# A two-layer network in fp32: the seven products per pair in another order, results formed in PSUM, a ninth piece of W, and the mixing, transposes and returns laid out by rows

## The chip, the cores and the metric

The kernel runs on one core of one Trainium2 chip. The time is the device time of one execution in microseconds. Before the change it is 2397.4 us, the median of two runs (2396.65 and 2398.15).

## The reference, cut to what matters

512 tokens of width 2048 pass through two layers. Layer 0 (forgetting attention and an RWKV-7 mixer) isn't touched. Layer 1 and the gate that closes it are:

```python
xn = rms_norm(h, norm_pre[i])
proj = xn @ c_w_in[j]                       # 512x2048 @ 2048x6144
u, v, g = _split(proj, (GMLP_W, GMLP_W, GMLP_W))
oc = chunked_spatial_gating(u, v, ...)      # below
y = (oc * jax.nn.silu(g)) @ c_w_out[j]
h = h + rms_norm(y, norm_post[i])
h = h + (p[i] @ ple_w_proj[i]) * jax.nn.sigmoid(h @ ple_w_gate[i])

# chunked_spatial_gating: 4 chunks of 128 tokens, 16 groups of 128 channels
u = gelu(u); v = layer_norm(gelu(v), ln_g, ln_b)
mixed = einsum('gts,bnsgc->bntgc', w_s * causal, vc) + b_s
return u * mixed
```

All of it is fp32 and the result must keep fp32's precision.

## The kernel before, in words

**Precise products.** Each fp32 operand is split into a high part `hi` (a ScalarE cast to the reduced format) and a low part `lo` (VectorE, the difference), and each product takes three matmuls: hi·hi, hi·lo, lo·hi. The two casts of a weight block are `whi` (line 1303) and `wlo` (line 1304) in the products that this change touches; four buffers of each lie between them and TensorE.

**Seven products.** `h @ W` of layer 1 and the last gate `h @ ple_w_gate` are done by a Strassen-Winograd scheme (`seven`, line 1309). The 512 tokens are split in two halves of 256, the 2048 input channels in two halves, and two column blocks of 512 of W form a `Pair`. Instead of eight quarter products there are seven, numbered 1 to 7, each of 8 k-steps of 128 channels; a k-step is 6 matmuls of 128x128 by 128x512 (lines 1324 to 1326), a product 48. Token-side sums (A11, A12, A22, S1 to S4) are formed once by `sets` (line 1203). Weight-side sums are formed in place, in `pieces` of W (two k-steps, 512 KB, line 1251):

- 1 loads W11 and, where `keep` is set, leaves it in `pr.E`; 2 loads W21.
- 5 adds W12 to E by an accumulating DMA that GpSimd issues (line 1281).
- 6 loads W22 into `pr.H` and adds it to E on VectorE (line 1267); 3 uses H as it is.
- 7 adds W12 to H by an accumulating DMA (line 1292); 4 loads W21 once more into a piece of its own and adds it to E on VectorE.

`piece` and `gone` (lines 1241 to 1249) take pieces from a queue `raws` of eight buffers and put them back at its end. Products 1 and 2 share one accumulator in PSUM, as do 5 and 3; all accumulators, transposes and mixing results come from the eight PSUM banks named `mm`. After each product `seven` copies or combines accumulators into SBUF tiles named `comb` (four, lines 1331 to 1351) and hands each finished 128x512 result to `pr.emit`.

**Order.** `FIRST` (line 74) orders the 14 products of two interleaved pairs: b1, a1, b2, a2, then 5, 6, 3, 7, 4 of a, and the same of b. `NEXT` (line 78) orders one pair alone: 1, 5, 2, 6, 3, 7, 4. In `layer_c` (line 1366) the columns of v come first (V, 14 products, `FIRST`), then U0, G0, U1, G1 (seven each, `NEXT`): u of the first 1024 channels, its gate g, and the same of the other half. In `last_layer` (line 1101) the gate `ple_w_gate` is 14 products in the order of `FIRST`. A label such as G0.2 is product 2 of G0; a and b are the two pairs of a `FIRST`.

**Emits of layer 1.** `vals` (line 1375) applies Gelu, collects the layer norm's statistics and stores v to DRAM (`vd`) on SyncE's queue. `gates` applies Gelu into `u[n]`, `silu` (line 1390) multiplies Silu(g) into it, and for the first half stores it to DRAM (`yd2`). `mix` (line 1399) does one group's spatial mixing: three small loads into the one buffer `accq` and a load of v's group into an `sq` tile, normalising by four ScalarE instructions (line 1411), the mask and two multiply-adds on GpSimd (lines 1406, 1414, 1415), a transpose of the mixing weight (line 1417), the casts of the weight (1419) and of v (1423, 1424) into `sg` tiles, three matmuls (1427 to 1429) and the multiplication into `u` (1431). `done` (line 1463), called after each product, calls two mixes after each of the first four products of G0 and G1, and in G1 also `early` (line 1458): load four blocks of y from `yd2`, transpose them on TensorE and split them (`operands`, line 1442). The other eight `operands` come after the last product, ahead of `c_w_out`.

**The last layer.** `post_norm` (line 989) runs `c_w_out` through `dense_all` (line 970) and forms the norm's factor; the `filler` meanwhile runs `p @ ple_w_proj`, copies each result through an `sg` tile (line 1133) and stores it to DRAM (`pd`, line 1134). `late` then updates h and `flip` (line 1152) turns it to token rows, 16 times: four transposes (line 1156), a copy into an `sg` tile (line 1158), a store to DRAM (`rd`, line 1159). Only then come the token-side sums and the 14 products; `emit` (line 1173) loads the matching tiles of `pd` and `rd` (lines 1183, 1184), applies the sigmoid, multiplies, adds and stores the output (line 1188).

**What sets the order.** The code is written as a flow of tiles. A planner gives each engine one fixed order of instructions, by program order as priority, by its own estimate of when operands and buffers are there, and by `high_priority` blocks (the casts of W and the additions of pieces stand in one). On the chip each engine and each queue works through its order strictly and waits on semaphores. All plain DMAs are issued by SyncE's queue (SP); the accumulating ones by GpSimd.

Of the kernel before, what the change touches and what calls it, by code (L numbers as in the profile page):

```python
# [16 lines left out]
P = 128  # L17
T = 512
# [51 lines left out]
def f(ap):  # L70
# [3 lines left out]
FIRST = lambda a, b: [  # L74
    (b, 1, False), (a, 1, True), (b, 2, True), (a, 2, True),
    *[(pr, n, True) for pr in (a, b) for n in (5, 6, 3, 7, 4)],
]
NEXT = 1, 5, 2, 6, 3, 7, 4


class Pair:


    def __init__(self, W, c0, n, emit):
        self.W, self.c0, self.n, self.emit = W, c0, n, emit
        self.E, self.H, self.acc, self.R = {}, {}, {}, {}


class Net:
# [899 lines left out]
    def post_norm(self, wap, gname, ops, keep, ps, wp, early, filler, kts=None):  # L989
# [3 lines left out]
        for n, acc in self.dense_all(wap, 0, ops, ps, 3, None, kts):  # L993
# [11 lines left out]
    def run(self):  # L1005
        tc = self.tc
        with ExitStack() as ctx:
# [12 lines left out]
            self.homes = {}  # L1020
            self.ahead = {}
# [6 lines left out]
    def rest(self, cp):  # L1028
        nc, tc, i = self.nc, self.tc, self.i
        npre, npost = self.cols["norm_pre"], self.cols["norm_post"]  # L1030
        with ExitStack() as ctx:
# [66 lines left out]
            pops = self.layer_c(cp, sets, accq, after, wp, ps)  # L1098
            self.last_layer(cp, pops, wp, ps)

    def last_layer(self, cp, yops, wp, ps):
# [36 lines left out]
        self.post_norm(i["c_w_out"][0], npost[:, 16:32], yops, keep, ps, wp, early, filler())  # L1138
# [13 lines left out]
        def flip(g, m):  # L1152
# [6 lines left out]
            nc.sync.dma_start(self.rd[:, m, g * T : (g + 1) * T], o)  # L1159

        def late(q):
            update(q, 1)
            update(q + 4, 1)
            if q % 2:
                for g in (q // 2, q // 2 + 2):
                    for m in range(4):
                        flip(g, m)

        sets = self.sets(A11, H, ps, wp, lambda q: (("yh", 2 * q + 8), ("yh", 2 * q + 9)), False, late)

        spare = []

        def emit(pr, m, n, src, cs=slice(0, T)):
            sg = src
            if not spare:
                for j in (2, 3):
                    tl = self.t(self.xp, [P, 4, T], f"xh{j}")
                    spare.extend(tl[:, q, :] for q in range(4))
            if (m, n % 2) in ((0, 0), (1, 0)):
                sg = self.t(wp, [P, T], "sg")  # L1180
            pj, res = self.t(wp, [P, T], "sq"), spare[0]
            spare.append(spare.pop(0))
            nc.sync.dma_start(pj, self.pd[:, m, n * T : (n + 1) * T])
            nc.sync.dma_start(res, self.rd[:, m, n * T : (n + 1) * T])
            nc.scalar.activation(sg, src, AF.Sigmoid)
            nc.vector.tensor_tensor(sg, sg, pj, ALU.mult)
            nc.vector.tensor_tensor(res, res, sg, ALU.add)
            nc.sync.dma_start(self.out[0, m * P : (m + 1) * P, n * T : (n + 1) * T], res)
# [3 lines left out]
        self.seven(FIRST(*pairs), sets, ps)  # L1192
# [10 lines left out]
    def sets(self, A11, xs, ps, wp, place, copy, late=lambda q: None):  # L1203
# [7 lines left out]
        A22, S3 = [[], []], [[], []]  # L1211
# [4 lines left out]
        for q in range(4):  # L1216
# [13 lines left out]
            self.part(S3, q, t)  # L1230
            src = xs[q + 4, 1]
            if copy:
                src = tmp("sg")
                nc.scalar.copy(src, xs[q + 4, 1])
            for e, (k, n) in enumerate(place(q)):
                A22[e].append(pair(k, n))
            self.part(A22, q, src)
        return {1: A11, 2: A12, 3: S4, 4: A22, 5: S1, 6: S2, 7: S3}

# [8 lines left out]
    def gone(self, tl):  # L1248
        self.raws.append(self.homes.pop(id(tl))[0])

    def pieces(self, pr, prod, keep):
# [8 lines left out]
        def load(*where):  # L1260
            tl = self.piece()
            nc.sync.dma_start(view(tl), block(*where))
            return tl

# [4 lines left out]
        for j in range(4):  # L1269
# [7 lines left out]
            elif prod == 5:  # L1277
# [3 lines left out]
                nc.gpsimd.dma_start(view(tl), block(0, 1, j), accum_op=ALU.add)  # L1281
# [6 lines left out]
            elif prod == 3:  # L1288
                tl = pr.H[j]
            elif prod == 7:  # L1290
                tl = done = pr.H.pop(j)
                nc.gpsimd.dma_start(view(tl), block(0, 1, j), accum_op=ALU.add)
            else:
# [3 lines left out]
                self.gone(g)  # L1297
# [11 lines left out]
    def seven(self, order, sets, ps, after=lambda n: None):  # L1309


        nc = self.nc
        for step, (pr, prod, keep) in enumerate(order):
# [4 lines left out]
            hs, ls = sets[prod]  # L1318
            for k, hi, lo in self.pieces(pr, prod, keep):
                for m in range(2):  # L1320
                    ms = slice(m * P, (m + 1) * P)
                    xh, xl = hs[k // 2][:, k % 2, ms], ls[k // 2][:, k % 2, ms]
                    more = dict(skip_group_check=True)
                    nc.tensor.matmul(acc[m], xh, hi, start=(first and k == 0), stop=False, **more)  # L1324
                    nc.tensor.matmul(acc[m], xh, lo, start=False, stop=False, **more)  # L1325
                    nc.tensor.matmul(acc[m], xl, hi, start=False, stop=(k == 7), **more)  # L1326
            tile = lambda: self.t(self.rp, [P, 2, T], "comb")
            for m in range(2):
                a = acc[m]
                if prod in (1, 5):  # L1330
                    if m == 0:
                        pr.R[prod] = tile()
                    nc.scalar.copy(pr.R[prod][:, m], a)
# [5 lines left out]
                elif prod == 7:  # L1339
                    if m == 0:  # L1340
                        pr.R[7] = tile()
                    u2, u3, c22 = (pr.R[x][:, m] for x in (1, 7, 5))
                    nc.vector.tensor_tensor(u3, a, u2, ALU.add)
# [432 lines left out]
```

## Time and profile before

| what | value |
|---|---|
| median of the runs | 2397.4 us |
| the profiled execution, its own time | 2392.33 us |
| its span, first to last instruction | 2390.6 us |
| mean granted clock | 0.972 |
| V's first product starts | 1384.6 us |
| first matmul of `c_w_out` | 1973.7 us |
| first product of the last layer starts | 2197.4 us |
| last matmul starts | 2379.4 us |

The profile is of one execution. PE is TensorE, PEld its weight loads, DVE VectorE, ACT ScalarE, POOL GpSimd, SP SyncE with its DMA queue. A stage is a stretch of the span between the starts of two products. "A <- B: t, n, m" in the views of waits says that A waited for B t us in all, n times, at most m us. In a group, "x16 | 23.0, 1435 | 2.3" is a count, the busy us, the mean ns of one and the idle us of that engine just before. In the timeline a line starts with the start and the length in us; what stands in brackets is the idle time ahead of it and who ended it.

### The profile page before, as it was taken

How to read it: one execution, taken by the hardware profiler on the slowest of the kernel's cores; microseconds unless marked ns; L12 is line 12 of the kernel's file. 1: busy time of each engine (PE TensorE's matmuls, PEld its weight loads, DVE VectorE, ACT ScalarE, POOL GpSimd, SP SyncE). 2: the span in 40 equal slices, each digit the busy share in tenths (PEclk: the TensorE clock that was granted, in tenths of full speed). 3: DMA queues.
4: the chain of work that ended last, by engine and by line, in shares of the span. 5: the costliest groups of instructions: out<-in, count | busy, mean ns of one | idle time of the engine just before them, and what ended most of it. 6: DMA issues, size and time to landing. Idle time of an engine off the chain costs nothing.

```text
span 2390.6 us, 39003 instructions
## 1 busy us (share of the span) xinstructions
PE 2263.8 (95%) x14787; PEld 1840.4 (77%) x14787; DVE 1463.8 (61%) x2817; ACT 1229.4 (51%) x2510; POOL 280.3 (12%) x334
## 2 busy tenths in 40 slices
PE   8999999999999999999999999998798689998977
PEld 7878888888887888788888887776576468886756
DVE  8667666676447778832374496765576563235957
ACT  5455555555446777722454474464454443345734
POOL 2010101101000000000101111021402210010010
PEclk9999999999999999999999999999899799998989
DMA  6332222222337333432344466665467364335695
GB/s 224 85 83 75 80 73 79 81 72 63 94 96 207 97 100 101 126 115 96 105 150 132 124 180 175 181 143 159 122 194 179 100 171 151 97 106 192 171 245 158
DMA packets 297881, 309.49 MB, mean 129 GB/s; under 512 B 14637, under 2 KB 198094, under 8 KB 296670
## 3 DMA queue, kind: packets, MB, share of 16 engines
q1 hardware_dynamic: 280286, 273.45, 37.3%
q0 software_dynamic: 17408, 33.56, 8.3%
q8 instruction: 116, 1.90, 0.3%
q14 instruction: 71, 0.58, 0.1%
HBM read 272.06 MB, written 34.90 MB: 128 GB/s over the span
## 4 chain that ended last, share of the span: by engine, by line
PE 70%; DMA 12%; DVE 8%; ACT 4%; issue 3%; POOL 1%; SPq 0%; ACTq 0%; POOLq 0%; DVEq 0%
PE mm L195 11%; PE mm L197 10%; PE mm L196 10%; PE mm L981 6%; PE mm L982 6%; PE mm L983 6%; PE mm L1325 4%; PE mm L1326 4%; PE mm L1324 4%; DVE wlo L1304 3%; DMA rq<-in_c_w_in_dram 3%; PE tm L533 1%; ACT whi L1303 1%; DMA accq<-in_c_ln_g_dram 1%; DMA rq<-in_ple_w_gate_dram 1%
## 5 line engine op out<-in xcount | busy, mean ns | idle before, releaser
L181 DVE TENSOR_TENSOR wlo<-raw,whi 128x512 fp32r<-128x512 f32 x464 | 331.9, 722 | 425.4 <-ACT whi L179 385.8
L179 ACT CAST whi<-raw 128x512 fp32r<-128x512 f32 x464 | 287.4, 621 | 453.0 <-PE mm L982 223.4
L196 PE MATMUL mm<-xl,whi 128*128 128x512 f32 x1088 | 427.3, 393 | 0.0
L195 PE MATMUL mm<-xh,whi 128*128 128x512 f32 x1008 | 418.7, 415 | 0.0
L197 PE MATMUL mm<-xh,wlo 128*128 128x512 f32 x1008 | 398.5, 395 | 0.0
L1303 ACT CAST whi<-rq 128x512 fp32r<-128x512 f32 x332 | 203.4, 619 | 173.0 <-PE mm L1326 101.5
L1304 DVE TENSOR_TENSOR wlo<-rq,whi 128x512 fp32r<-128x512 f32 x332 | 227.0, 695 | 102.2 <-ACT whi L1303 101.5
L196 PEld LDWEIGHTS mm<-xl,whi 128*128 128x128 f32 x1088 | 205.6, 189 | 33.7
L197 PEld LDWEIGHTS mm<-xh,wlo 128*128 128x128 f32 x1008 | 189.5, 188 | 42.0
L195 PEld LDWEIGHTS mm<-xh,whi 128*128 128x128 f32 x1008 | 190.3, 189 | 33.8
L983 PE MATMUL mm<-yl,wlo 128*128 128x512 f32 x336 | 130.7, 389 | 0.0
L981 PE MATMUL mm<-yl,whi 128*128 128x512 f32 x336 | 130.7, 389 | 0.0
L1363 POOL TENSOR_TENSOR accq<-accq,sq 128x512 f32<-128x512 f32 x42 | 56.8, 1353 | 531.4 <-ACT sq L1361 530.3
L1324 PE MATMUL mm<-whi,yl 128*128 128x512 f32 x256 | 105.3, 411 | 14.0 <-ACT whi L1303 14.0
L1325 PE MATMUL mm<-wlo,yh 128*128 128x512 f32 x256 | 104.0, 406 | 15.1 <-DVE wlo L1304 15.0
L1303 ACT CAST whi<-raw 128x512 fp32r<-128x512 f32 x116 | 71.5, 619 | 80.4 <-PE mm L1326 46.7
L982 PE MATMUL mm<-xl,whi 128*128 128x512 f32 x288 | 112.0, 389 | 0.0
L1304 DVE TENSOR_TENSOR wlo<-raw,whi 128x512 fp32r<-128x512 f32 x116 | 81.9, 712 | 42.4 <-ACT whi L1303 42.3
L1325 PE MATMUL mm<-wlo,yl 128*128 128x512 f32 x256 | 104.8, 409 | 1.1 <-DVE wlo L1304 0.9
L1324 PE MATMUL mm<-whi,yh 128*128 128x512 f32 x256 | 101.8, 398 | 3.2 <-ACT whi L1303 3.2
L1326 PE MATMUL mm<-whi,yl 128*128 128x512 f32 x256 | 103.8, 405 | 0.0
L1324 PE MATMUL mm<-whi,xl 128*128 128x512 f32 x256 | 101.9, 398 | 0.0
(484 smaller groups left out, 4770.5 us busy)
## 6 DMA issues: line engine op xcount, KB each, us to landing
raw<-in_ab_w_in_dram SPq DMA_DIRECT2D x128, 512.0 KB, 3.9
rq<-in_c_w_in_dram SPq DMA_DIRECT2D x72, 512.0 KB, 6.3
raw<-in_ple_w_gate_dram SPq DMA_DIRECT2D x36, 512.0 KB, 3.8
rq<-in_c_w_in_dram POOLq DMA_DIRECT2D x36, 512.0 KB, 6.7
raw<-in_ab_w_out_dram SPq DMA_DIRECT2D x32, 512.0 KB, 3.7
rq<-in_ple_w_gate_dram SPq DMA_DIRECT2D x32, 512.0 KB, 6.8
raw<-in_c_w_out_dram SPq DMA_DIRECT2D x32, 512.0 KB, 3.8
raw<-in_c_w_in_dram SPq DMA_DIRECT2D x28, 512.0 KB, 5.0
```

The source lines that it names most:

```text
L179: nc.scalar.copy(hi[:, : m * n], src)
L181: self.weng.tensor_tensor(lo[:, : m * n], src, f(hi[:, : m * n]), ALU.subtract)
L195: nc.tensor.matmul(acc, hi, xhi[k], start=(k == 0), stop=False)
L196: nc.tensor.matmul(acc, hi, xlo[k], start=False, stop=False)
L197: nc.tensor.matmul(acc, lo, xhi[k], start=False, stop=(k == nk - 1))
L981: nc.tensor.matmul(accs[j], hi[:, js], xhi[k], start=(k == 0), stop=False)
L982: nc.tensor.matmul(accs[j], hi[:, js], xlo[k], start=False, stop=False)
L983: nc.tensor.matmul(accs[j], lo[:, js], xhi[k], start=False, stop=(k == nk - 1))
L1303: nc.scalar.copy(hi, src)
L1304: nc.vector.tensor_tensor(lo, src, f(hi), ALU.subtract)
L1324: nc.tensor.matmul(acc[m], xh, hi, start=(first and k == 0), stop=False, **more)
L1325: nc.tensor.matmul(acc[m], xh, lo, start=False, stop=False, **more)
```

## The change

- `NEXT` becomes 1, 2, 5, 6, 3, 4, 7. `FIRST` becomes b1, a1, b2, a2, then a: 5, 6, 3, 4, 7, then b: 5, 6 and 3, 4, 7 (in the last layer 7, 4, 3, where product 3 loads W22 once more).
- `raws` holds nine pieces instead of eight; `comb` three tiles instead of four. The piece of product 4's second load goes back to the front of the queue instead of its end.
- Results are formed in the accumulators: product 3's emit works on PSUM, as do Silu and the sigmoid; 4 and 7 are combined when both are done.
- At three places (`hold`) the matmuls of two or three k-steps are grouped by accumulator half.
- `later` and `tick` put steps at a k-step's end. Each `mix` is split into load, norm, split and mul, at k-steps -11, -7, 0 and +3 of a mark; marks lie 6.4 k-steps apart; the parameters alternate between `accq` and `rstdB`. Early transposes get their load five k-steps ahead, into tiles `yl`. The last eight `operands` move into the first row of `c_w_out` (`pre`). Flips come one to a k-step in the last layer's first two products. `pd` and `rd` are loaded ahead of the product that needs them (`fetch`), and the output store is issued two k-steps after its sum.
- The stores to `vd`, `yd2` and `rd` are issued by ScalarE.

```diff
-FIRST = lambda a, b: [
+FIRST = lambda a, b, end=(3, 4, 7): [
     (b, 1, False), (a, 1, True), (b, 2, True), (a, 2, True),
-    *[(pr, n, True) for pr in (a, b) for n in (5, 6, 3, 7, 4)],
+    *[(a, n, True) for n in (5, 6, 3, 4, 7)], *[(b, n, True) for n in (*NEXT[2:4], *end)],
 ]
-NEXT = 1, 5, 2, 6, 3, 7, 4
+NEXT = 1, 2, 5, 6, 3, 4, 7
...
-            self.raws = deque([(self.wraw, "raw", 2)] * 2 + [(wq, f"rq{j}", 1) for j in range(6)])
-            self.rp = pool("rp", 4)
+            self.raws = deque([(self.wraw, "raw", 2)] * 2 + [(wq, f"rq{j}", 1) for j in range(7)])
+            self.rp = pool("rp", 3)
...
-            nc.sync.dma_start(self.rd[:, m, g * T : (g + 1) * T], o)
+            nc.scalar.dma_start(self.rd[:, m, g * T : (g + 1) * T], o)
...
+        for k, (g, m) in enumerate((g, m) for g in (2, 0, 3, 1) for m in range(4)):
+            self.later(k, lambda g=g, m=m: flip(g, m))
+        self.later(16, rest)
...
+        def fetch(n, ms):
+            for m in ms:
+                pj[n, m], res[n, m] = (x[0] for x in spare)
+                for x in spare:
+                    x.append(x.pop(0))
+                nc.sync.dma_start(pj[n, m], self.pd[:, m, n * T : (n + 1) * T])
+                nc.sync.dma_start(res[n, m], self.rd[:, m, n * T : (n + 1) * T])
+
+        def emit(pr, m, n, src):
+            nc.scalar.activation(src, src, AF.Sigmoid)
+            nc.vector.tensor_tensor(src, src, pj[n, m], ALU.mult)
+            o = res[n, m]
+            nc.vector.tensor_tensor(o, o, src, ALU.add)
+            self.later(
+                2, lambda: nc.sync.dma_start(self.out[0, m * P : (m + 1) * P, n * T : (n + 1) * T], o)
+            )
...
+        order = FIRST(*pairs, (7, 4, 3))
...
+    def gone(self, tl, first=False):
+        home = self.homes.pop(id(tl))[0]
+        (self.raws.appendleft if first else self.raws.append)(home)
+
+    def later(self, n, step):
+        self.todo.append((self.clock + n, len(self.todo), step))
+        self.todo.sort(key=lambda x: x[0])
+
+    def tick(self):
+        self.clock += 1
+        while self.todo and self.todo[0][0] <= self.clock:
+            self.todo.pop(0)[2]()
...
             elif prod == 3:
-                tl = pr.H[j]
+                if j in pr.H:
+                    tl = pr.H[j]
+                else:
+                    tl = done = load(1, 1, j)
...
                 g = load(1, 0, j)
                 add(tl, g)
-                self.gone(g)
+                self.gone(g, True)
...
+            hold = {1: (6,), 2: (0,)}.get(prod, ())
+            if step == len(order) - 1:
+                hold = 5, 6
...
+                elif prod == 3:
+                    nc.vector.scalar_tensor_tensor(a, a, -1.0, pr.R[1][:, m], ALU.mult, ALU.subtract)
+                    pr.emit(pr, m, pr.n + 1, a)
+            pr.done.add(prod)
+            if prod == 7:
+                u3 = pr.R[7] = pr.R[1] if 3 in pr.done else self.t(self.rp, [P, 2, T], "comb")
+                for m in range(2):
+                    nc.vector.tensor_tensor(u3[:, m], acc[m], pr.R[1][:, m], ALU.add)
+                    c22 = pr.R[5][:, m]
+                    nc.vector.tensor_tensor(c22, c22, u3[:, m], ALU.add)
                     pr.emit(pr, 2 + m, pr.n + 1, c22)
+            if prod in (4, 7) and {4, 7} <= pr.done:
+                for m in range(2):
+                    u = pr.R[7][:, m]
+                    nc.vector.tensor_tensor(u, pr.acc[4][m], u, ALU.subtract)
+                    pr.emit(pr, 2 + m, pr.n, u)
...
+            nc.scalar.dma_start(self.vd[:, m, n * T : (n + 1) * T], dst)
             nc.vector.bn_stats(st[:, m, n, :], dst)
-            nc.sync.dma_start(self.vd[:, m, n * T : (n + 1) * T], dst)
...
-            par = self.t(wp, [P, T], "accq", bufs=1)
...
+                par = self.t(wp, [P, T], "accq", bufs=1) if g % 2 else self.rstdB
...
+            for n, step in ((-11, load), (-7, norm), (0, split), (3, mul)):
+                self.later(at + n, step)
...
             for j in range(2):
-                at = step - nv - 14 * j - 7
-                if 0 <= at < 4:
-                    mix(8 * j + 2 * at)
-                    mix(8 * j + 2 * at + 1)
...
+                if step == nv + 14 * j + 1:
+                    for e in range(8):
+                        mix(8 * j + e, 5 * 8 + 3 + int(6.4 * e))
+            if step == nv + 13:
+                for n in range(2):
+                    self.later(4, lambda n=n: saved(n))
+            if step == nv + 21:
+                for n in range(8):
+                    early(n, (14, 18, 22, 26, 31, 35, 39, 43)[n])
...
-        for n in range(8, KT):
-            operands(n, lambda m, n=n: u[n // 4][:, m, n % 4 * P : n % 4 * P + P])
-        return yops
+        def pre(k):
+            for n in range(8, 11) if k == 0 else range(10 + k, min(11 + k, KT)):
+                last(n)
```

More of the change, by code (lines that the diff above doesn't have):

```diff
@@ L1020, in run @@
             self.homes = {}
+            self.clock, self.todo = 0, []
             self.ahead = {}
@@ L1163, in late @@
             update(q + 4, 1)
[L1164 to L1169, printed above, removed]
-        spare = []
[L1173 to L1188, printed above, removed]
+        sets = self.sets(A11, H, ps, wp, None, False, late)
@@ new lines, in ahead @@
+        def ahead(step):
+            if step + 1 < len(order):
+                pr, prod, _ = order[step + 1]
+                if prod == 2:
+                    fetch(pr.n, (0, 1))
+                elif prod == 3:
+                    fetch(pr.n + 1, (0, 1))
+                elif prod == 7:
+                    fetch(pr.n + 1, (2, 3))
+                    if 4 in pr.done:
+                        fetch(pr.n, (2, 3))
+                elif prod == 4 and 7 in pr.done:
+                    fetch(pr.n, (2, 3))
@@ L1194, in whole_set @@
+        self.seven(order, sets, ps, ahead)
+        self.clock += 100
+        self.tick()
     def whole_set(self):
@@ L1318, in seven @@
             hs, ls = sets[prod]
+            hold = {1: (6,), 2: (0,)}.get(prod, ())
+            if step == len(order) - 1:
+                hold = 5, 6
+            rows = []
             for k, hi, lo in self.pieces(pr, prod, keep):
[L1320 to L1327, printed above, removed]
+                rows.append((k, hi, lo))
+                if k not in hold:
+                    for m in range(2):
+                        ms = slice(m * P, (m + 1) * P)
+                        for r, hi, lo in rows:
+                            xh, xl = hs[r // 2][:, r % 2, ms], ls[r // 2][:, r % 2, ms]
+                            more = dict(skip_group_check=True)
+                            nc.tensor.matmul(acc[m], xh, hi, start=(first and r == 0), stop=False, **more)
+                            nc.tensor.matmul(acc[m], xh, lo, start=False, stop=False, **more)
+                            nc.tensor.matmul(acc[m], xl, hi, start=False, stop=(r == 7), **more)
+                    rows = []
+                self.tick()
             for m in range(2):
@@ L1456, in operands, with early, load, saved @@
             yops[0][n], yops[1][n] = hi, lo
-        def early(n):
-            y = self.t(wp, [P, 4, P], "sq")
-            nc.sync.dma_start(y, self.yd2[:, :, n * P : (n + 1) * P])
-            operands(n, lambda m: y[:, m, :])
+        def early(n, at):
+            own = {}
+            def load():
+                y = own["y"] = self.slot("yl", n, F32).rearrange("p (m c) -> p m c", c=P)
+                nc.sync.dma_start(y, self.yd2[:, :, n * P : (n + 1) * P])
+            self.later(at - 5, load)
+            self.later(at, lambda: operands(n, lambda m: own["y"][:, m, :]))
+        def saved(n):
+            for m in range(4):
+                nc.scalar.dma_start(self.yd2[:, m, n * T : (n + 1) * T], u[n][:, m, :])
         def done(step):
-            if step == 1:
+            if step == 0:
                 pc = self.t(ps, [P, 4, 2], "mm")
```

169 lines of the change are left out of this document (89 added, 80 removed).

## The prediction

> **What bounds the kernel now.** First the page: TensorE is busy nearly throughout, but the slices show holes and a lower granted clock in the last third only.
>
> ```profile
> span 2390.6 us, 39003 instructions
> PE   8999999999999999999999999998798689998977
> PEclk9999999999999999999999999999899799998989
> ```
>
> So I cut the part that the change touches into its own stages, by the first matmul of each product (line 1324): nine products of V and its last five, then U0, G0, U1, G1 (seven each), the last operands of y, and in the last layer the gap ahead of its products, its first four, its other ten, and the tail. Columns: stretch, length, busy time and instructions of PE, PEld, DVE, ACT, POOL, granted clock, DMA share, GB/s.
>
> ```profile
> 1384.62:1487.40 102.78, 100.23 (x442) 81.81 (x441) 85.25 (x132) 67.64 (x118) 13.27 (x12) 1.00 0.67 170
> 1487.40:1552.74 65.34, 57.13 (x242) 45.70 (x240) 44.29 (x65) 29.16 (x49) 6.91 (x6) 0.95 0.71 196
> 1552.74:1634.43 81.69, 78.61 (x337) 62.46 (x336) 57.12 (x86) 49.53 (x88) 12.52 (x10) 1.00 0.68 174
> 1634.43:1755.45 121.02, 96.42 (x370) 73.83 (x368) 71.53 (x104) 59.90 (x118) 36.74 (x33) 0.87 0.55 146
> 1755.45:1833.20 77.75, 77.09 (x338) 62.82 (x337) 53.41 (x78) 42.16 (x70) 8.76 (x8) 1.00 0.67 171
> 1833.20:1967.36 134.16, 100.99 (x397) 77.89 (x396) 72.43 (x107) 58.44 (x110) 31.10 (x29) 0.83 0.51 129
> 1967.36:1973.70 6.34, 4.62 (x31) 3.30 (x29) 6.34 (x12) 4.49 (x9) 0.00 (x0) 1.00 0.97 312
> 2173.10:2197.40 24.30, 13.87 (x66) 10.73 (x64) 12.19 (x21) 9.55 (x17) 0.00 (x0) 0.70 0.59 209
> 2197.40:2247.78 50.38, 48.45 (x192) 39.02 (x193) 35.84 (x59) 31.82 (x58) 4.78 (x4) 0.91 0.74 203
> 2247.78:2379.40 131.62, 115.65 (x481) 93.06 (x479) 96.32 (x143) 58.88 (x99) 14.46 (x12) 0.94 0.69 187
> 2379.40:2390.65 11.25, 0.14 (x1) 0.00 (x0) 7.26 (x12) 2.46 (x4) 0.00 (x0) 0.71 0.51 182
> ```
>
> U1 is the yardstick: nothing but its 336 matmuls at clock 1.00, so 77.75 / 7 = 11.11 us a product and 77.75 / 336 = 0.231 us a matmul. Against it the rest loses: V 2.8 and 9.8 us, U0 3.9, G0 43.3, G1 56.4, the last operands 6.3, the last layer 24.3 + 6.0 + 20.5 and an 11.25 us tail: 184.5 us. TensorE sets the end, and what it waits for is to be read stage by stage. In G0 and G1, where the mixing runs (first two rows from G0, next two from G1), and who is behind ScalarE there (the last three, from the waits of ScalarE and GpSimd from 1384 us on):
>
> ```profile
> PE mm L1427 <- ACT sg L1423: 10.6, 3, 5.3
> PE mm L1427 <- ACT w L1419: 6.0, 4, 2.1
> PE mm L1427 <- ACT sg L1423: 22.4, 5, 6.5
> PE mm L1445 <- DMA sq<-yd: 6.2, 4, 3.1
> ACT sg L1423 <- POOL sq L1415: 35.8, 15, 5.2
> POOL accq L1406 <- DMA accq<-in_c_w_s_dram: 51.8, 13, 12.0
> POOL sq L1414 <- ACT sq L1411: 37.0, 5, 15.1
> ```
>
> The mixing matmuls stand in TensorE's order before their chain (load, normalise, GpSimd, cast) is through, and with one `accq` buffer the next load starts only when the last mix has used it. The rest of the loss is lower clock after those holes (0.87 and 0.83).
>
> **The mixing by rows.** The change emits each mix in four parts, load, norm, split and matmul, 11 and 7 k-steps before and 3 after the split, one mix each 6.4 k-steps, with two parameter buffers. A k-step is 11.11 / 8 = 1.39 us: 8.9 us between mixes, 9.7 us from norm to split, 4.2 us from split to matmul.
>
> ```profile
> L1415 POOL TENSOR_TENSOR sq<-sq,accq 128x512 f32<-128x512 f32 x16 | 23.0, 1435 | 2.3 <-DMA accq<-in_c_ln_b_dram 1.2
> L1414 POOL TENSOR_TENSOR sq<-sq,accq 128x512 f32<-128x512 f32 x16 | 21.8, 1360 | 53.8 <-ACT sq L1411 37.0 <-DMA accq<-in_c_ln_g_dram 12.8 <-issue 2.2
> L1411 ACT ACTIVATE sq<-sq,nb,rv 128x128 f32<-128x128 f32 x64 | 28.5, 487 | 8.1 <-DMA sq<-vd 7.9 <-DVE nb L1479 0.2
> 2173.10 1.03 PE L1156 MATMUL mm<-ident,yh 128*128 128x128 f32 x8
> ```
>
> Norm is 4 x 0.487 + 1.36 + 1.44 = 4.7 us plus the select, under 9.7. The work stays: three matmuls and a transpose, 3 x 0.231 + 1.03 / 8 = 0.82 us for each of 16 mixes, 13.1 us, and 32 early transposes, 4.2 us. Stalls in G0 and G1: 43.3 + 56.4 - 17.3 = 82 us. What remains lies between 0 (some mixes wait for nothing even now) and the 1.2 us that a mix waits here when its chain is ready and only the copy of its own transpose is late:
>
> ```profile
> 1670.05 0.50 PE L1427 MATMUL mm<-sg,w 128*128 128x512 f32 x1 [1.19 <-ACT w L1419]
> 1677.51 0.50 PE L1427 MATMUL mm<-sg,w 128*128 128x512 f32 x1
> ```
>
> I take the middle, 0.6 us, 10 us in all. **Gain 72 (63 to 82; if half of the waits stay, 41).** The early transposes of y get their loads five k-steps (6.9 us) ahead and slots of their own, where a load now fights for the two `sq` buffers; they are in the 72. The last eight move into the first product row of `c_w_out`, whose first k-steps have operands already: of 6.34 us the 24 transposes keep 3.1. **Gain 3.**
>
> **Order and ninth piece.** Two rows of the DMA queues from 1380 us to the end (1011 us), one of the page (KB each, us to landing), and the waits at the two changes of pair:
>
> ```profile
> q1 hardware_dynamic: 90368, 127.70, 38.9%
> q0 software_dynamic: 17408, 33.56, 19.5%
> rq<-in_c_w_in_dram SPq DMA_DIRECT2D x72, 512.0 KB, 6.3
> 1496.91 0.79 PE L1324 MATMUL mm<-whi,yl 128*128 128x512 f32 x1 [6.62 <-ACT whi L1303]
> 2294.65 0.80 PE L1325 MATMUL mm<-wlo,yh 128*128 128x512 f32 x1 [6.47 <-DVE wlo L1304]
> ```
>
> A product's plain 2.1 MB take 0.389 x 1011 / 127.7 x 2.1 = 6.5 us of all DMA engines, an accumulated one 0.195 x 1011 / 33.56 x 2.1 = 12.3 us, longer than the 11.11 us that it feeds. Now 5 follows 1 and 7 follows 3 at once; in the new order a plain product or 4 stands between, so the accumulate has 11 us more. At V's change of pair that saves most of 9.8 us (the late loads of product 5), with the bias transpose out of the way: **gain 8 (3 to 12).** Against it: all four second loads of product 4 go through the ninth piece, which is handed back to the front: load 6.3, add 1.23, next load. Four take some 30 us; they may start in product 6 and have 22 us until 4 begins and 8 more until its last piece, so they just fit, if VectorE's adds stand that early. Of U0's product 4 (from 1621.2) the adds now stand from 7 us ahead to 4.6 us into it, each as its load lands:
>
> ```profile
> 1613.96 1.23 DVE L1267 TENSOR_TENSOR rq<-rq,rq 128x1024 f32<-128x1024 f32 x1 [2.64 <-DMA rq<-in_c_w_in_dram]
> 1625.84 1.23 DVE L1267 TENSOR_TENSOR rq<-rq,rq 128x1024 f32<-128x1024 f32 x1 [1.39 <-DMA rq<-in_c_w_in_dram]
> ```
>
> An add that waits holds the `wlo` behind it and so TensorE; four weight buffers cover 5.6 us. I charge **4 us (0 to 152, the third rival).**
>
> In the last layer's ten products the order of the first pair helps likewise, but there the DMA is nearly full: plain 6 x 6.5 (one more than now, product 3 loads W22 again), accumulated 4 x 12.3, twelve result tiles of 0.79 MB at 3.1 us/MB, 29: 117 us against 111 of TensorE. Around a3 to b5 it is 6.5 + 12.3 + 6.5 + 12.3 + some 15 of returns = 53 against 44. So of 20.5 us I leave 9. **Gain 11.5 (0 to 20).**
>
> **Returns and stores.** The gap is a chain of copies and stores through two `sg` buffers:
>
> ```profile
> 2183.13 1.22 ACT L1133 COPY sg<-mm 128x512 f32<-128x512 f32 x2 [2.93 <-DMA pd<-sg]
> 2188.58 1.25 ACT L1158 COPY sg<-mm 128x512 f32<-128x512 f32 x2 [1.48 <-DMA rd<-sg]
> 2191.31 1.24 ACT L1158 COPY sg<-mm 128x512 f32<-128x512 f32 x2 [1.47 <-DMA rd<-sg]
> L1303 ACT CAST whi<-rq 128x512 fp32r<-128x512 f32 x332 | 203.4, 619 | 173.0 <-PE mm L1326 101.5
> 1420.26 0.34 SPq L1383 DMA_DIRECT2D vd<-xh  x1
> ```
>
> Two flips take 2.73 us. Laid one to a k-step (1.39 us) between the matmuls of the first two products they need the same rate, but TensorE has work meanwhile. Of 24.3 + 6.0 = 30.3 us, the 64 transposes are 8.2. Of the 22 left I keep 10: the `pd` stores, unchanged, hold ScalarE until 2184, and a flip (1.24 / 2), its issue (0.34 on SP's queue, taken for ScalarE's too) and a cast (0.62) are 1.58 us a k-step, over 1.39. **Gain 12 (5 to 22).** Elsewhere ScalarE issues 24 more stores, 8 us over some 580 us at about half load (42.16 of 77.75 in U1), and they leave SP, where they stood ahead of loads of W. The Trainium skill, "DMA: Bandwidth & Descriptors", section "Issuing engines are not separate DMA queues", speaks against a gain from this: all transfers share the same 16 engines, and another issuer only saves issue time; by it the queue move alone is worth nothing, and my sum gives it nothing either.
>
> **Tail.** From the last matmul on, two emits with late `pj` loads take 11.25 us; the last result is added here:
>
> ```profile
> 2386.48 0.69 DVE L1187 TENSOR_TENSOR xh<-xh,comb 128x512 f32<-128x512 f32 x1
> ```
>
> From its end to the span's end is 3.5 us and stays. Combine, sigmoid, multiply, add in PSUM with operands already there: 0.69 + 0.62 (as a cast) + 0.69 + 0.69 and hand-overs, 3.5. **Gain 4 (2 to 6).** In-PSUM results otherwise save no time on TensorE.
>
> **Sum:** 72 + 3 + 8 - 4 + 11.5 + 12 + 4 = 106.5. The profiled execution took 2392.3 us (span 2390.6 and 1.7 around it): 2286. The median of the runs is 5.1 us higher, 2397.4: **2291 us.**
>
> **Rivals.** (1) Only half of the mixing's waits go: the planner sets each engine's order by costs of its own, and where GpSimd or a load is later than it reckons (the 35.8 and 51.8 us above), the cast and the matmul wait again. Gain 106.5 - 31, 2322 us, or 2333 with the last layer's DMA gain lost too. Against it: 4.7 us of work has 9.7. (2) Nearly all waits go: 82 + 3 + 12 + 20 + 22 + 6 = 145, 2252 us. For it: U1 runs so now; against it, the last layer's DMA. (3) **Slower**, by the ninth piece alone: if the adds of product 4 stay in product 4, as load and add stand side by side in the code, its four loads run one by one, 4 x (6.3 + 1.23) = 30.1 us against 11.1; eight such products lose 152 us, less 106.5: 2443 us, at the very edge of two per cent. It decides once 4's lead of 22 us shrinks by more than 13. Against it: adds carry the casts' priority, and the rows show them where their loads land. (4) ScalarE's in-order stores hold the casts behind them: 40 stores, each waiting as long as a flip's copy now pays for a pair, 1.48, plus 0.34 to issue, lose 73 us: 2364 us. Against it: each store stands right behind its own producer. The Trainium skill, "TensorE: Matmul & The Clock Gate", section "Architectural detail: the array is 16× 32×32, not 1× 128×128", calls ScalarE's queue strict FIFO, which is what this rival needs; no row here shows a store on it.
>
> **How the numbers follow.** Forecast 0.60, (1) 0.19, (2) 0.10, (3) 0.05, (4) 0.06. Its own range is 2265 to 2315; to hold eight in ten it takes in (1) and most of (2): 2245 to 2345. Two per cent, about what a measurement here tells from no change, is 48 us, to 2349: faster is forecast, (1) and (2), 0.89; (4) and half of (3), which lies on the edge, are within it, 0.08; the other half is slower by more, 0.03.
>
> **What would show it.** Right: G0 and G1 each at 85 to 95 us with clock near 1.00 and the waits at the mixing's first matmul under 1 us each; b5 of V near 12 us; the first product of the last layer starting within 3 us of the last `ple_w_proj` matmul; 7 us of tail; one stall left about the last layer's b5. Wrong: product 4 longer than 13 us with VectorE's add waiting for a load; ScalarE waiting for stores; mixing waits of 3 us and more.

## The result, and the profile after

The changed kernel takes **2323.2 us** (median of 2 runs, 2323.08 to 2323.41) against 2397.4: a ratio of 0.969, 95% interval 0.965 to 0.973. The forecast was 2291 (2245 to 2345). So it is faster, in the range, and gains 74 us where the sum said 106.5. The profiled execution took 2323.4 us.

The page of the changed kernel, span, busy tenths of TensorE and its clock in 40 slices (the prediction shows the same three lines of before):

```profile
span 2321.7 us, 39023 instructions
PE   9999999999999999999999999999979989996898
PEclk9999999999999999999999999999999989999899
```

The holes of the last third are fewer, and one has got deeper, in slice 37. The same cuts as in the prediction, by the first matmul of a product (now line 1380): V's first nine products, its other five, U0, G0, U1, G1, then the last layer's first product, its next three, its other ten, and the tail:

```profile
1384.27:1484.65 100.38, 99.63 (x442) 81.95 (x441) 85.07 (x130) 67.91 (x118) 15.21 (x13) 1.00 0.73 188
1484.65:1540.52 55.87, 54.70 (x242) 44.97 (x240) 43.95 (x67) 29.23 (x48) 5.68 (x5) 1.00 0.76 218
1540.52:1618.96 78.44, 77.74 (x338) 62.60 (x336) 60.03 (x83) 48.51 (x85) 18.99 (x15) 1.00 0.71 182
1618.96:1724.01 105.05, 90.51 (x370) 69.23 (x368) 74.23 (x101) 55.66 (x111) 33.62 (x30) 0.95 0.65 159
1724.01:1806.84 82.83, 78.23 (x338) 62.60 (x337) 57.83 (x80) 45.17 (x75) 13.37 (x11) 1.00 0.66 173
1806.84:1914.21 107.37, 94.98 (x408) 75.25 (x406) 79.61 (x112) 59.09 (x113) 26.80 (x24) 0.92 0.70 178
2115.10:2156.02 40.92, 18.05 (x85) 13.20 (x83) 37.69 (x62) 24.35 (x42) 2.41 (x2) 0.76 0.48 138
2156.02:2196.92 40.90, 39.08 (x172) 30.98 (x173) 19.77 (x29) 24.92 (x43) 2.39 (x2) 0.94 0.87 266
2196.92:2314.99 118.07, 111.78 (x481) 90.69 (x479) 93.02 (x138) 55.78 (x94) 14.39 (x12) 0.99 0.81 222
2314.99:2321.70 6.71, 0.16 (x1) 0.00 (x0) 2.87 (x5) 0.58 (x1) 0.00 (x0) 0.69 0.20 78
```

Term by term, from these rows and those of before:

| part | before | after | gain | forecast |
|---|---|---|---|---|
| V, 14 products | 168.1 | 156.25 | 11.9 | 8 |
| U0 to G1, with mixing and transposes (72 + 3 - 4) | 421.0 | 373.7 | 47.3 | 71 |
| `c_w_out` and `ple_w_proj` (199.4 before, 200.9 after) | | | -1.5 | 0 |
| gap and first four products of the last layer | 74.7 | 81.8 | **-7.1** | 12 |
| its other ten | 131.6 | 118.1 | 13.6 | 11.5 |
| tail | 11.25 | 6.7 | 4.5 | 4 |

Two terms fail, the mixing by 24 us and the returns by 19. What TensorE waits for from V to the end shows both; line 1157 is a flip's transpose, 1159 its copy, 1380 and 1381 are matmuls with `whi` and `wlo`, 1498 is a mixing matmul:

```profile
PE mm L1157 <- ACT sg L1159: 21.5, 5, 18.6
PE mm L1380 <- ACT whi L1352: 19.4, 7, 7.6
PE mm L1381 <- DVE wlo L1353: 15.0, 19, 3.0
PE mm L1498 <- DVE sg L1492: 4.1, 2, 2.3
```

The mixing matmuls' own waits, 39 us in the three groups that the prediction shows, are down to 4.1: that step came as forecast. But from U0 to G1 TensorE now waits for casts of W, 19.4 us for `whi` and 7.5 for `wlo`, where the kernel before has 2.3 and 5.1, and one flip waits 18.6 us at a stretch.

**Who holds the casts.** The waits of ScalarE from 1540 to 1930 us have one large row from a load (7.9 us in the kernel before, in the prediction's row of line 1411). The timeline shows one of the two longest, in product 4 of G0; the other, 12.3 us, is in product 4 of G1:

```profile
ACT sq L1476 <- DMA sq<-vd: 53.9, 10, 12.3
```

```profile
1675.55 1.20 POOL L1309 DMA_DIRECT2D rq<-in_c_w_in_dram  x1
...
1682.74 0.53 SPq L1467 DMA_DIRECT2D sq<-vd  x1
1684.71 1.21 POOL L1309 DMA_DIRECT2D rq<-in_c_w_in_dram  x1 [1.14 <-DVE wlo L1353]
1694.17 0.49 ACT L1476 ACTIVATE sq<-sq,nb,rv 128x128 f32<-128x128 f32 x1 [11.70 <-DMA sq<-vd]
1695.23 0.79 PE L1380 MATMUL mm<-whi,yh 128*128 128x512 f32 x1 [6.78 <-ACT whi L1352]
```

The norm (1476) stands in ScalarE's order ahead of a cast. Its load of `vd` is issued at 1682.74 and lands some 11 us later, beside four accumulating loads issued from 1675.55 to 1684.71. ScalarE waits 11.70 us for it, and TensorE 6.78 for the cast behind it. The Trainium skill, "TensorE: Matmul & The Clock Gate", section "Architectural detail: the array is 16× 32×32, not 1× 128×128", calls ScalarE's queue strict FIFO; these two rows agree, and the holder is a load, not a store.

**Who holds the flip.** At the same place of the last layer:

```profile
2132.00 0.39 PE L1382 MATMUL mm<-whi,xh 128*128 128x512 f32 x1
2150.31 0.59 ACT L1159 COPY sg<-mm 128x512 f32<-128x512 f32 x1
2150.95 1.11 PE L1157 MATMUL mm<-ident,yh 128*128 128x128 f32 x4 [18.56 <-ACT sg L1159]
```

Two of the four sums of each operand set (lines 1243 and 1249) pass through the same two `sg` tiles as the flips. They are emitted first and keep the tiles until 2150, and the first flip's copy runs only then. Until 2128 TensorE has turned six flips, and with b1's two accumulators they hold all eight PSUM banks. The first row is b1's last matmul. The next flip's transposes, which have no bank, stand ahead of a1's matmuls on TensorE, and so it is 40.92 us from b1's first matmul to a1's.

### The profile page after: what moved, and what is told of

Read it like the earlier page. It is cut to its first block, busy times and chain, and to the rows that moved or that the text cites. A ratio compares the mean times of both kernels' runs of the same rounds, so it can differ in the third digit from the quotient of the medians.

```text
span 2321.7 us, 39023 instructions
## 1 busy us (share of the span) xinstructions
PE 2237.6 (96%) x14787; PEld 1823.7 (79%) x14787; DVE 1480.6 (64%) x2817; ACT 1229.2 (53%) x2510; POOL 284.8 (12%) x334
## 4 chain that ended last, share of the span: by engine, by line
PE 76%; DMA 9%; DVE 9%; ACT 3%; issue 2%; SPq 0%; POOL 0%; ACTq 0%; DVEq 0%
PE mm L195 11%; PE mm L197 11%; PE mm L196 11%; PE mm L982 6%; PE mm L983 6%; PE mm L981 6%; PE mm L1381 5%; PE mm L1382 5%; PE mm L1380 5%; DVE wlo L1353 3%; DMA sq<-vd 2%; DMA rq<-in_ple_w_gate_dram 2%; PE tm L533 1%; DMA rq<-in_c_w_in_dram 1%; PE tm L554 1%
## 5 line engine op out<-in xcount | busy, mean ns | idle before, releaser
L181 DVE TENSOR_TENSOR wlo<-raw,whi 128x512 fp32r<-128x512 f32 x464 | 331.8, 722 | 423.3 <-ACT whi L179 383.8
L179 ACT CAST whi<-raw 128x512 fp32r<-128x512 f32 x464 | 287.3, 620 | 455.9 <-PE mm L982 222.4
L1353 DVE TENSOR_TENSOR wlo<-rq,whi 128x512 fp32r<-128x512 f32 x336 | 240.9, 728 | 121.2 <-ACT whi L1352 120.8
L1380 PE MATMUL mm<-whi,yh 128*128 128x512 f32 x256 | 103.2, 403 | 14.8 <-ACT whi L1352 14.8
L1381 PE MATMUL mm<-wlo,xl 128*128 128x512 f32 x256 | 101.6, 397 | 4.3 <-DVE wlo L1353 4.0
L1380 PE MATMUL mm<-whi,yl 128*128 128x512 f32 x256 | 101.2, 395 | 3.5 <-ACT whi L1352 2.8
L1382 PE MATMUL mm<-whi,yh 128*128 128x512 f32 x256 | 101.9, 398 | 0.0
L1382 PE MATMUL mm<-whi,yl 128*128 128x512 f32 x256 | 100.7, 393 | 0.0
```

Of the source, the lines that this page charges most:

```text
L179: nc.scalar.copy(hi[:, : m * n], src)
L181: self.weng.tensor_tensor(lo[:, : m * n], src, f(hi[:, : m * n]), ALU.subtract)
L1353: nc.vector.tensor_tensor(lo, src, f(hi), ALU.subtract)
L1380: nc.tensor.matmul(acc[m], xh, hi, start=(first and r == 0), stop=False, **more)
L1382: nc.tensor.matmul(acc[m], xl, hi, start=False, stop=(r == 7), **more)
```

## The experiments

All were measured beside the kernel before on the same chip; `e1` to `e11` are changes of the changed kernel.

**The flips get their own tile (e1_flip_tiles).** Theory: the shared `sg` tiles cause the 18.6 us. Rival: it moves elsewhere, since the last layer's DMA is full.

```diff
-            o = self.t(wp, [P, T], "sg")
+            if not turned:
+                turned.append(self.t(self.rp, [P, 2, T], "comb"))
+            o = turned[0][:, m % 2]
```

> The flips of the last layer copy into the two halves of a free comb tile instead of the two sg tiles that the token-side sums use as well; nothing else is changed. Theory A (TensorE's 18.6 us wait at line 1157 is a queue for sg: the sums were handed the tiles first and the flips' transposes stand ahead of the matmuls in TensorE's order): the last layer's first product takes 14 to 22 us instead of 40.9, the time falls by 16 to 22 us, to 2301 to 2307. Rival B (ScalarE is simply overfull with casts of W, casts of the sums and copies of flips, some 34 us of work in 22): the wait spreads over the first four products and less than 6 us is won, 2317 to 2323.

Measured 2306.35 us, ratio 0.962 (0.960 to 0.965): 17 us less. Rows of the last layer's first product, its next three, its other ten:

```profile
2115.44:2133.11 17.67, 15.71 (x84) 12.42 (x85) 16.51 (x28) 11.45 (x21) 1.11 (x1) 1.00 0.77 267
2133.11:2172.10 38.99, 37.13 (x175) 29.50 (x174) 34.77 (x56) 30.80 (x57) 3.69 (x4) 1.00 0.86 225
2172.10:2297.18 125.08, 113.84 (x481) 91.47 (x479) 97.61 (x146) 59.46 (x100) 14.39 (x12) 0.96 0.83 233
```

b1 falls from 40.9 to 17.7 us: the cause is shown. But the last ten rise from 118.1 to 125.1: 7 of some 25 us are given back. Product 4 of pair a alone takes 18.9 us instead of 10.9: there an addition on VectorE waits 6.39 us for a second load, and the `wlo` behind it come late.

**The norm held behind a cast (e2_norm_held), and on GpSimd (e2g_norm_pool).** Theory: the norm ahead of the casts is what the mixing still costs. In the first, it is emitted four k-steps later and tied behind the cast that is current then; in the second it leaves ScalarE.

```diff
-                for m in range(4):
-                    nc.scalar.activation(
+                with tc.issue_after(self.cast.ins):
+                    for m in range(4):
+                        nc.scalar.activation(
...
-            for n, step in ((-11, load), (-7, norm), (0, split), (3, mul)):
+            for n, step in ((-11, load), (-3, norm), (0, split), (3, mul)):
```

> Each mix's four normalising instructions are emitted 3 k-steps ahead of its split instead of 7 and tied behind ScalarE's cast of that k-step, so that they can't be pulled ahead; loads, buffers and pieces stay. Theory A (the norm stands in ScalarE's order a few us behind the issue of its load, waits 54 us in all for it, and the casts of W behind it wait too): the waits at line 1476 fall from 54 us to under 15, products 4 of G0 and G1 fall from 23.5 and 25.7 to 11 to 14 us, the time falls by 20 to 35 us, to 2288 to 2303. Rival C (the stalls in products 4 come from the single ninth piece through which all second loads pass): products 4 stay above 20 us and less than 6 us is won, 2317 to 2323.

Measured 2305.3 us, ratio 0.962 (0.960 to 0.965), 18 us less and 2 us above the expected range. ScalarE's waits in the same window, then product 4 of G0 and of G1 with the norm held:

```profile
ACT sg L1492 <- POOL sq L1482: 36.6, 14, 5.9
...
ACT sq L1477 <- DMA sq<-vd: 4.1, 2, 2.1
```

```profile
1686.60:1701.68 15.08, 12.30 (x54) 9.44 (x52) 8.51 (x15) 6.85 (x15) 3.32 (x5) 1.00 0.87 242
1865.41:1878.75 13.34, 13.09 (x63) 10.46 (x62) 11.46 (x18) 9.06 (x19) 2.91 (x2) 1.00 0.97 278
```

53.9 us of waits for `vd` become 4.1; the two products take 15.1 and 13.3 us, 23.5 and 25.7 in the changed kernel. The new row on top is the price: with four k-steps fewer, GpSimd is sometimes late for the split, and TensorE's waits for the mixing rise from 4.1 to 15.1 us.

```diff
-                    nc.scalar.activation(
-                        vn[:, m, :], vn[:, m, :], AF.Identity, bias=nb[:, m : m + 1], scale=rv[:, m : m + 1]
+                    nc.gpsimd.tensor_scalar(
+                        vn[:, m, :], vn[:, m, :], rv[:, m : m + 1], nb[:, m : m + 1], ALU.mult, ALU.add
```

> The four normalising instructions of each mix run on GpSimd (multiply and add with the two per-token columns) instead of ScalarE; order marks, loads and pieces stay. Theory A: ScalarE no longer waits for a load of v at all and the casts of W flow, 15 to 30 us are won, 2293 to 2308, if GpSimd's waits don't hold its accumulating DMAs too long. Rival C (the ninth piece): no more than 6 us, 2317 to 2323. If GpSimd's own queue becomes the trouble, products 5 and 7 grow and the time is 2323 to 2350.

Measured 2314.8 us, 0.967 (0.965 to 0.969), less of a gain than expected: off ScalarE the wait for `vd` is on GpSimd, 63.1 us in ten waits, and GpSimd issues the accumulating loads of W: product 5 of U0 takes 15.1 us (11.3 in the changed kernel), product 7 of G0 19.7 (13.6).

**Both causes taken away (e5_both):** e1 and e2 in one kernel.

> The flips get their tile of comb and the norm is held behind a cast, both in one kernel. A, two separate causes: the last layer's first product loses its 18.6 us wait at the flips and G0.4 and G1.4 lose their 10 us waits, each as when done alone; the sum of the two savings (17 and 18 us) is 35, so 2284 to 2293 us. B, the last layer takes back what comes early because its DMA is full: no more than the better of the two alone, 2298 to 2306 us.

Measured **2285.6 us**, ratio 0.954 (0.953 to 0.956), the fastest of all, and the gains add. G0, G1 (short of its last 1.4 us), the last layer's first four, its other ten:

```profile
1616.08:1715.48 99.40, 89.16 (x369) 71.23 (x368) 75.42 (x103) 57.24 (x114) 36.09 (x32) 0.95 0.68 174
1791.64:1891.19 99.55, 91.64 (x396) 73.68 (x395) 84.25 (x110) 60.11 (x120) 35.67 (x29) 0.95 0.76 196
2094.64:2149.41 54.77, 52.35 (x256) 42.05 (x257) 49.65 (x82) 41.27 (x77) 4.80 (x4) 1.00 0.84 248
2149.41:2275.26 125.85, 115.17 (x481) 92.26 (x479) 98.93 (x147) 60.26 (x102) 14.43 (x12) 0.96 0.82 231
```

**The ninth piece returned to the end (e3_piece_end).** Product 4's second load goes back behind the other pieces, as before.

```diff
-                self.gone(g, True)
+                self.gone(g)
```

> The piece of product 4's second load goes back to the end of the queue as before the change, so that the third and fourth second load can use pieces freed by product 4 itself. Theory A (loads of v hold ScalarE): no change beyond 5 us either way, 2318 to 2328. Rival C (ninth piece holds products 4): products 4 of G0 and G1 fall to 12 to 16 us and 15 to 25 us are won, 2298 to 2308.

Measured 2337.0 us, 0.976 (0.974 to 0.978): 14 us slower than the changed kernel, neither theory's figure, and the intervals lie apart. TensorE's waits for `whi` from V to the end are 26.3 us, 12 times, against 19.4 us, 7 times. Products 4 of G0 and G1 do fall, from 23.5 and 25.7 us to 18.6 and 18.5, but those of V, U0 and U1 rise from 10.9 to between 15.8 and 18.9. Handing the piece back to the front, which the prediction feared, is better than the end.

**The stores on SP's queue again (e4_stores_sp).**

```diff
-            nc.scalar.dma_start(self.rd[:, m, g * T : (g + 1) * T], o)
+            nc.sync.dma_start(self.rd[:, m, g * T : (g + 1) * T], o)
```

and likewise for `vd` and `yd2`.

> The stores of vd, yd2 and rd are issued on SP's queue again, all else as in the changed kernel. A, as the prediction's sum has it, another issuer is worth nothing: 2318 to 2329 us. B, on SP a store that waits for its producer holds the loads of W behind it: V (32 stores) and the last layer's first products show casts waiting for loads, 8 to 25 us more, 2331 to 2348 us. C, ScalarE's own issues hold its casts: SP is better, 2305 to 2315 us.

Measured 2322.3 us, 0.970 (0.968 to 0.972): nothing. SP's own waits over V (1384 to 1545 us; V has 16 stores, not the 32 of the expectation) show why. First with the stores on SP (1305 loads W, 1444 stores `vd`), then the changed kernel:

```profile
SPq L1305 <- DVE wlo L1353: 58.1, 24, 9.0
SPq L1305 <- DMA raw<-in_c_w_in_dram: 20.9, 5, 5.5
SPq L1444 <- ACT comb L1443: 19.1, 5, 6.8
SPq L1305 <- DVE rq L1313: 15.8, 7, 8.8
SPq L1444 <- ACT xh L1443: 12.7, 7, 5.6
```

```profile
SPq L1305 <- DVE wlo L1353: 68.1, 27, 9.0
SPq L1305 <- DMA raw<-in_c_w_in_dram: 37.8, 8, 10.2
SPq L1305 <- DVE rq L1313: 19.2, 7, 11.5
```

The stores wait 19.1 + 12.7 = 31.8 us on SP, and the waits of the loads fall by nearly as much, from 125.1 us in the three rows to 94.8: SP had that time to spare. The Trainium skill's rule that another issuer only saves issue time ("DMA: Bandwidth & Descriptors", section "Issuing engines are not separate DMA queues") agrees.

**The old order (e6_old_order), and the old order with eight pieces (e11_old_order_eight).** The last layer's second pair keeps 5 6 7 4 3 in both.

```diff
-    *[(a, n, True) for n in (5, 6, 3, 4, 7)], *[(b, n, True) for n in (*NEXT[2:4], *end)],
+    *[(a, n, True) for n in (5, 6, 3, 7, 4)], *[(b, n, True) for n in (5, 6, *end)],
-NEXT = 1, 2, 5, 6, 3, 4, 7
+NEXT = 1, 5, 2, 6, 3, 7, 4
```

and for e11 besides

```diff
-            self.raws = deque([(self.wraw, "raw", 2)] * 2 + [(wq, f"rq{j}", 1) for j in range(7)])
+            self.raws = deque([(self.wraw, "raw", 2)] * 2 + [(wq, f"rq{j}", 1) for j in range(6)])
```

> The seven products in the old order again (1 5 2 6 3 7 4, and both pairs in turn 5 6 3 7 4; the last layer's second pair keeps 5 6 7 4 3), all else as in the changed kernel. A, an accumulated load needs more than one product's time and so stalls at the changes of pair and in the last layer: V loses 8 to 10 us, the last layer 5 to 12, U0 and G0 a few: 2336 to 2350 us. B, the order is worth nothing by itself (U1 lost nothing in the old order): 2318 to 2330 us.

> The old order of the products, and eight pieces of W in place of nine. The old order with nine took 2328 us and lost nothing in V. A, the ninth piece is what took the waits at the changes of pair: V is back near 165 us with product b5 at 16 us or more, G0 and G1 lose more, 2340 to 2360 us. B, V's gain came from elsewhere (the bias transpose moved away, stores off SP's queue): 2323 to 2334 us.

Measured 2328.2 us, 0.972 (0.970 to 0.975), and 2357.5 us, 0.984 (0.983 to 0.986). The order alone is worth 5 us here, with an interval that overlaps the changed kernel's; the ninth piece, in the old order, 29. V, first with nine pieces and then with eight:

```profile
1382.78:1539.51 156.73, 155.10 (x682) 126.76 (x681) 131.79 (x202) 98.11 (x168) 20.57 (x18) 1.00 0.76 201
```

```profile
1384.70:1558.02 173.32, 158.20 (x683) 127.38 (x681) 132.38 (x202) 96.65 (x167) 19.89 (x17) 0.98 0.69 182
```

V keeps its whole gain in the old order (156.7 against 156.25) and loses it, and 5 us more (173.3 against 168.1 before), with eight pieces. The bias transpose is moved in both. What the ninth piece changes is when the second loads of product 4 can start. The first addition for product 4 of V's pair a, which starts at 1472.39 us with nine pieces and at 1474.39 with eight, in the same order:

```profile
1439.60 1.22 DVE L1313 TENSOR_TENSOR rq<-rq,raw 128x1024 f32<-128x1024 f32 x1
1467.16 1.23 DVE L1313 TENSOR_TENSOR rq<-rq,raw 128x1024 f32<-128x1024 f32 x1 [1.60 <-DMA raw<-in_c_w_in_dram]
```

It is 32.8 us ahead of its product with nine and 7.2 us with eight. The loss is not where it was before, though. With eight, product 4 of pair a takes 21.0 us in V and 34.1 in the last layer, against 12.6 and 10.9 in the kernel before, and b5 of V 12.9 against 19.4. e11 keeps the return of the piece to the front, as before the change it went to the end, so the 29 us are those of the ninth piece together with that return; eight pieces with the return to the end were not run in the changed kernel. In the last ten products TensorE's largest group of waits grows as well, first with nine, then with eight:

```profile
PE mm L1381 <- DVE wlo L1353: 8.3, 4, 5.2
```

```profile
PE mm L1380 <- ACT whi L1352: 17.5, 3, 10.7
```

**What took the mixing's waits: parts laid by rows, spacing, or the second parameter buffer (e7 to e10).** In e7 the four parts of a mix come at one k-step; in e8 two mixes stand together at the end of a product as well; e9 is e7, and e10 is e8, with one parameter buffer.

```diff
-            for n, step in ((-11, load), (-7, norm), (0, split), (3, mul)):
+            for n, step in ((0, load), (0, norm), (0, split), (0, mul)):
```

in all four; for e8 and e10 also the first edit here, for e9 and e10 the second:

```diff
-                        mix(8 * j + e, 5 * 8 + 3 + int(6.4 * e))
+                        mix(8 * j + e, 48 + 8 * (e // 2))
...
-                par = self.t(wp, [P, T], "accq", bufs=1) if g % 2 else self.rstdB
+                par = self.t(wp, [P, T], "accq", bufs=1)
```

> Load, norm, split and matmul of a mix are issued at one k-step (the split's), still one mix each 6.4 k-steps and with two parameter buffers. A, the rows are what took the mixing's waits: G0 and G1 are back near their old 43 and 56 us of waits, 2360 to 2385 us. B, spreading one mix each 6.4 k-steps and the second parameter buffer did most of it: less than 16 us more, 2320 to 2339 us.

> As the run with the four parts at one k-step, but two mixes together at the end of each of the first four products of G0 and G1, where the kernel before has them; still two parameter buffers. A, the spacing of one mix each 6.4 k-steps took the waits: G0 and G1 lose 15 to 30 us more each, 2345 to 2375 us. B, the second parameter buffer took them: 2310 to 2328 us.

> Mixes in pairs, four parts at once, and one parameter buffer: all three as in the kernel before, in the changed kernel. A, rows, spacing and buffer together are the whole of the mixing's gain: G0 and G1 lose near their old 43 and 56 us, 2355 to 2380 us. B, part of the gain came from elsewhere (y loaded into slots of its own, the sum of order and pieces): 2325 to 2345 us.

> One mix each 6.4 k-steps, its four parts at one k-step, and one parameter buffer: with the runs before it this fills the square of spacing and buffer (spaced with two 2315, pairs with two 2318, pairs with one 2350). A, the second buffer alone is what counts, since a load of parameters takes as long to land however the mixes stand: 2338 to 2352 us. B, with 8.9 us between mixes one buffer is free again in time, so that spacing and buffer each do it alone: 2312 to 2330 us.

| four parts at once | two buffers | one buffer |
|---|---|---|
| one mix each 6.4 k-steps | e7 2315.1 (0.967, 0.965 to 0.969) | e9 2325.3 (0.971, 0.969 to 0.973) |
| two mixes per product | e8 2318.5 (0.968, 0.967 to 0.970) | e10 2350.1 (0.981, 0.980 to 0.983) |

TensorE's waits from 1540 to 1960 us with mixes in pairs, two buffers and then one (1486 is the transpose of a mix, 1497 and 1499 its matmuls):

```profile
PE mm L1497 <- ACT w L1488: 12.5, 8, 4.3
PE mm L1499 <- DVE w L1489: 9.0, 4, 3.4
```

```profile
PE mm L1497 <- ACT sg L1491: 23.3, 8, 4.6
PE mm L1497 <- ACT w L1488: 16.0, 4, 7.1
PE mm L1486 <- POOL accq L1479: 12.2, 6, 3.3
```

21.5 us against 51.5. Theory A of e7 fails: with load, norm, split and matmul emitted at one k-step nothing is lost. That doesn't bring the parts together on the chip, since the planner moves them: the mix that is loaded at 1669.29 us in the changed kernel has its cast at 1696.25 and its first matmul at 1704.09, and in e7 it is loaded at 1672.70, cast at 1689.21 and multiplied at 1706.87. So the marks are not what took the waits; what parts that really stand together would cost was not measured. Two buffers or a mix each 8.9 us is enough, and only with neither do the waits come back. With one buffer the spacing still leaves some 10 us (e9 against e7). e10 lies between its two theories' ranges. Its G0 takes 123.9 us, and its G1, up to the last matmul:

```profile
1816.82:1942.98 126.16, 98.77 (x403) 76.90 (x402) 73.00 (x112) 59.44 (x113) 30.47 (x29) 0.88 0.61 155
```

With 121.0 and some 135 before and 105.1 and 107.0 in the changed kernel, by the same cut, spacing, buffer and marks together are some 38 of the 44 us that the two stages gained. e10's G0 lies 3 us above that of before and its G1 9 us below; those 9, in the stage where y is also loaded and turned, were not taken apart.

## Why the prediction was right and where it failed

**The bound.** Right: TensorE sets the end, and the gain came from the stages named. Of the signs, b5 of V (10.9 us), the start of the last layer right behind `ple_w_proj` and the tail came; G0 and G1 took 105 and 107 us instead of 85 to 95. Two of its readings are slightly off: U1, the yardstick of 11.11 us a product, has 1.5 us of waits in it (a product without waits takes 10.88), and G1's last matmul starts at 1968.17, so that 1 of the 6.3 us of the last operands is G1's.

**Mixing, 72 us: the wrong queue was checked.** U0 to G1 gained 47.3 of 71. The step "Norm is 4 x 0.487 + 1.36 + 1.44 = 4.7 us plus the select, under 9.7" held for norm to split: the mixing matmuls hardly wait, although the marks did not set the distance (in the trace the norm starts 8 to 26 us ahead of the cast, and up to 102 us for the first mixes of G0 and G1). It left out the stretch ahead of it, load to norm, and what stands behind the norm on ScalarE: the casts of W. This is the place of rival (1), a load later than the planned order reckons and then cast and matmul waiting, but its victim is W's matmul, not the mix's. With the norm held (e2) 18 us come back, and in e5 it is 353.1 us from U0's first matmul (1539.92) to the first of `c_w_out` (1892.97), a gain of 68 against the 71 of the sum.

Also wrong is the credit: "The mixing by rows" was given the whole term. Emitted at once or by rows is the same time within the intervals (2315 and 2323), and what removes the waits is the second buffer or the spacing. By rows and with the norm held it is 10 us less (2305 against 2315), but the norm was not held with the parts at once, so what rows add there is not shown.

**Order and ninth piece: size right, cause wrong.** V's 8 us came as 11.9, but "the accumulate has 11 us more" is not why: the old order keeps V's gain. The ninth piece, charged 4 us with a rival at 152, is what wins, by e6 and e11. Products 4 of V, U0 and U1 now take 10.88 us each, and so does b5 of V, which is no wait at all; the row is product 4 of U0:

```profile
1597.20:1608.08 10.88, 10.88 (x50) 9.01 (x48) 6.65 (x11) 6.16 (x10) 0.00 (x0) 1.00 1.08 293
```

By this row rival (3) is dead. The prediction counted the DMA time of a product and not how early its load may start. E and H of a pair hold eight pieces, so with eight in all the second loads of product 4 wait until product 7 gives pieces back, however free the DMA is: 7.2 us ahead of the product instead of 32.8. (In the new order product 4 comes while 7 still needs its four pieces; there the ninth was not taken away, so its 29 us holds for the old order, with the return to the front.)

**Last ten products, 11.5:** 13.6 measured, again by pieces rather than order: in the old order TensorE's largest group of waits there is 8.3 us with nine pieces and 17.5 with eight.

**Returns, 12: sign wrong in the changed kernel.** "They need the same rate, but TensorE has work meanwhile" failed. The work stood behind the flips in TensorE's order, and the flips behind the sums in the two `sg` tiles. With a tile of their own the gap and first four products take 54.8 us (e5) against 74.7, a gain of 20 where 12 was forecast. Part of it is given back in the last ten (125.9 against 118.1); e1's waits there are for `wlo` of product 4 and later, behind an addition that waits for its load. That the fuller DMA is why the load is late is only argued.

**Queue move, 0, and rival (4):** right by e4; ScalarE's waits for stores, 11.6 us, lie at the flips' and `pd`'s copies, and in V it has 0.3 us of them. **Tail, 4:** 4.5.

That the time fell on rival (1)'s 2322 is partly chance: between the profiled executions 68.9 us were gained of 106.5; of the 37.6 missing, 24 are of its kind, in another place, and 19 the flips, less some 6 that V and the last ten gained over the sum. With both faults out, e5's 2285.6 lies near the 2291 of the forecast, though two of its terms earned it by other means.

## What to carry to other kernels

When an instruction is moved early, ask not only whether its own chain has time but what stands behind it on its in-order engine if its input is late. Count buffers before you count transfer time: a second parameter buffer was worth some 30 us with mixes in pairs, and a ninth piece of W as much in the old order with the return to the front, while the new order of products was worth 5 or nothing that stands clear of the intervals. Marks in the program are priorities, not times: read from the trace where the parts came to stand. Two uses of one small ring of tiles are tied in the order in which they are emitted, and a transpose whose PSUM bank waits for such a tile stops every matmul behind it.

## What the runs showed of the hardware

Loads of layer 1's W landed later in the faster kernel: the medians from issue to landing, of plain and accumulating loads into the `rq` pieces, were 6.3 and 6.7 us before and are

```profile
rq<-in_c_w_in_dram SPq DMA_DIRECT2D x75, 512.0 KB, 6.9
rq<-in_c_w_in_dram POOLq DMA_DIRECT2D x38, 512.0 KB, 8.5
```

after, with the DMA share of G1 up from 0.51 to 0.70. So a landing time taken from a trace full of holes need not hold in the kernel without them. It is no bound either: the plain loads of `ple_w_gate` into `rq` pieces went the other way, from 6.8 us to 5.1. The granted clock followed the holes as well: G0 and G1 at 0.87 and 0.83 before, 0.95 and 0.92 after, 0.95 in both with both causes removed (e5).
